# One decoder layer on one core: the residual's copy to DRAM in four pieces on the weights' queue, adding transfers in one half of down only, two results turned at other units

## The chip, the cores and the metric

One Trainium2 chip, of which the program uses one core. The metric is the device time of one execution in microseconds (us); the time of a kernel is the median of its timed runs.

## The reference, cut to what matters

The input is 256 tokens by 2048 numbers in float32. What matters here is the middle and the end of the layer: the residual `h` after attention, the SwiGLU block with its three weight matrices, and the gated block behind it.

```python
h = h + jnp.concatenate([out_mla, out_moba], axis=-1) @ w_o[i]

f = rmsnorm(h, ffn_norm[i])
h = h + (jax.nn.silu(f @ w_gate[i]) * (f @ w_up[i])) @ w_down[i]     # D_FF = 5632

g = jax.nn.sigmoid(rmsnorm(h, ple_norm[i]) @ w_ple_gate[i])
h = h + g * (p[i] @ w_ple_proj[i])
return rmsnorm(h, final_norm)
```

## The kernel before

**Products.** Every float32 operand is split into a high part (its value in the shorter format `fp32r`) and a low part (the rest), and a product is three matmuls (L342 to L344): high by high, low of the activations by high of the weights, high of the activations by low of the weights. The third one is the only one that reads the low part of the weights.

**Units and turns.** The work of TensorE is a list of units. A unit takes two blocks of 128 rows of a weight matrix by up to 1024 columns (1 MB). Some units have several turns. The groups of units come in this order: `wo0`, `wo1` (the product with `w_o`), then `g0`, `u0`, and for ci = 1 to 4 `g{ci}` (gate), `d{ci}0` (left half of the product with `w_down`, four units), `u{ci}` (up), `d{ci}1` (right half, four units), then `gu5`, `dl0`, `dl1` (the last piece of down, six units each) and the gated block (`pg`, `pe`). Five of the eight units of `g1` to `gu5` are done by Strassen's scheme in four turns, with seven products in place of eight and extra sums on VectorE (L330 to L334); `g1` and `u0` have fewer of these units.

**How a weight reaches TensorE.** SyncE's queue loads 1 MB into one of the buffers `raw` (L221), three of them until `wo1` and five after that: the fourth and the fifth lie where the attention results `oB` lie, which `wo1` reads to its end. ScalarE writes the high part from `raw` (`split_hi`, L317), VectorE the low part (`split_lo`, L325). Both go to a ring of places of 512 columns: 12 in the tiles `ringh`/`ringl`, 4 in `moreh`/`morel`, 4 in `most`. `plan` gives each split its places and the turn that read them last; the split is emitted right after that turn. `most` lies where `h` lies, so it may be used only while `h` is out of on-chip memory: from unit `wide + 8` (the first of `u0`; `wide` is the first of `g0`) up to `dl0`.

**The adding form of the low part.** For the unit with index 3 of each group of down, `split_hi` does something else: ScalarE writes the negative of `raw` into the low part's place (L315), a DMA on GpSimd's queue adds `raw` to it (L316), and ScalarE writes the high part. VectorE then has nothing to do for this unit.

```python
if units[jb.unit].adding:
    nc.scalar.mul(l, r, -1.0)
    nc.gpsimd.dma_start(l, r, accum_op=ALU.add)
nc.scalar.copy(h[:, :, c0:c1], r[:, :, c0:c1])
```

**The residual.** `h` is complete when `wo1` ends. `ffn_norm_half` scales it (L843), turns it with transposes on TensorE (L137) and splits it into `aT`, in steps between the units of `g0`. At the end of its second half a DMA on GpSimd's queue copies `h` (2 MB) to `hd` in DRAM (L863). Results of `d1` to `d4` are added to `hd` by DMAs on the same queue (L808), and `h` comes back in `dl0` (L993). GpSimd's queue also adds the Strassen sums to the gate's result (`stage<-U`, L903), once at the end of `g1` to `g4`, just ahead of the left half of down.

**Small steps.** `tasks` holds generators; at each even turn `step` runs those whose waiting count is over. The turned results of gate and up (`ff_transpose`, 8 transposes and two splits per step) are such a generator. For ci = 1 to 4 it is kept apart in `mid`, taken up when `d{ci}1` ends, and run at odd turns of the units that are not Strassen's: index 0 and index 1 of the next gate group.

Of the kernel before, what the change touches and what calls it, by code (L numbers as in the profile page):

```python
# [34 lines left out]
def kernel(ctx, tc, x, p, positions, attn_norm, w_in, kv_norm, w_ukv, w_o, ffn_norm,  # L35
                             w_gate, w_up, w_down, ple_norm, w_ple_gate, w_ple_proj, final_norm,
                             inv_freq, out):
    nc = tc.nc
# [162 lines left out]
    RING = 12  # L201
# [31 lines left out]
    def plan(wide):  # L233

        last, at = {}, 0

        def job(i, kind, kks, places):
            nonlocal at
            u, jb = units[i], Job()
            jb.unit, jb.kind, jb.kks, jb.turn, jb.first = i, kind, kks, len(turns), None  # L240
            if u.store:
                jb.wait = len(turns) - 3
            else:
                top = (RING + 8 if wide + 8 <= i < back else RING + 4) if u.deep else RING
                while at >= top or any(at < x < at + places for x in (RING, RING + 4)) or at + places > top:
                    at = 0 if at + 1 >= top else at + 1
                jb.first = at
                jb.wait = max(last.get(x, -1) for x in range(at, at + places))
                for x in range(at, at + places):
                    last[x] = len(turns)  # L250
                at += places
            jobs.append(jb)
            return jb

        order = [0, 1, 2]
        back = next(i for i, u in enumerate(units) if u.name == "dl0")
        for i, u in enumerate(units):
            u.turns = []
            if u.again:
                continue  # L260
            if i == wide + 3:
                order = [3, 4] + order
            u.raw = order.pop(0)
            order.append(u.raw)
            nch, nk = len(u.chunks), len(u.ks)
            if u.strassen:
                todo = [[("11 22", (0,), 2)], [("21", (0,), 1)], [("t3 t1", (0,), 2)], [("t2 t4", (0,), 2)]]
            elif u.store or u.adding or not u.mixed:
                todo = [[("", tuple(range(nk)), nk * nch)]]
            else:  # L270
                todo = [[("", (kk,), nch)] for kk in range(nk)]
                if u.last:
                    todo = [[x for y in todo for x in y]]
            for t in todo:
                u.turns.append([job(i, *x) for x in t])
                turns.append(i)
# [139 lines left out]
    def add(gen, wait=0, front=False):  # L416
        tasks.insert(0 if front else len(tasks), [wait, gen])
# [143 lines left out]
    S = {"done": 0, "doneB": 0}  # L561
# [23 lines left out]
    def stage_tile(n):  # L585
        return big.tile([128, NT, n], F32, name="stage", tag="stage")
# [240 lines left out]
    def ffn_norm_half(k0):  # L827

        def after():
            def g():  # L830
                if k0 == 0:
                    S["nrm"] = stage_tile(1024).rearrange("q t (a b) -> q (t a) b", a=2).rearrange(
                        "q n (u v) -> q n u v", u=2)
                    S["sums"] = big.tile([128, 2, 4, 3, 128], F32R, name="sums", tag="att")
                    if SEVENS > 4:
                        S["sums4"] = big.tile([128, 2, SEVENS - 4, 3, 128], F32R, name="sums4", tag="tabs")
                    S["s4"] = big.tile([128, 2, 128], F32, name="s4", tag="vb")
                    S["s4b"] = big.tile([128, SEVENS - 2, 128], F32, name="s4b", tag="mask")
                    S["rs"] = make_rstd(ssh[:, :, 0:2], D // 2, "rs")
                    yield 1  # L840
                def scale(k):
                    for t in range(NT):
                        nc.scalar.mul(S["nrm"][:, (k // 2) % 2, t], S["h"][:, t, k * 128:k * 128 + 256], S["rs"][:, t:t + 1])  # L843

                scale(k0)
                if k0:
                    scale(k0 + 2)
                yield 1
                for k in range(k0, k0 + 8, 2):
                    sums = [*(sums_of(k, i) for i in range(2)), S["s4"][:, k // 2] if k < 4 else S["s4b"][:, k // 2 - 2]] if k // 2 < SEVENS else None  # L850
                    act_transpose(S["h"], k, G_FFN, aT, scaled=True, sums=sums)
                    nx = k + (4 if k0 else 2)
                    if nx < k0 + 8:
                        scale(nx)
                    if k == 8:
                        rf = make_rstd(ssh, D, "rf0")
                        S["rf"] = const.tile([128, NT], F32, name="rf")
                        nc.vector.reciprocal(S["rf"], S["rs"])
                        nc.vector.tensor_tensor(S["rf"], S["rf"], rf, op=ALU.mult)
                    yield 1  # L860
                if k0:
                    S["hd"] = dram.tile([128, NT, D], F32, name="hd")
                    nc.gpsimd.dma_start(S["hd"], S["h"])  # L863
            add(g(), 1 if k0 == 0 else 0)
        return after

# [44 lines left out]
    def up_evac(ci, n, nb):  # L911
        left = {"n": nb}

        def f(c, t, c0, c1, b, off=0):
            st = S["ff"][:, t, c0 - off:c1 - off]
            nc.vector.scalar_tensor_tensor(st, b, S["rf"][:, t:t + 1], st, op0=ALU.mult, op1=ALU.mult)
            left["n"] -= 1
            if left["n"] == 0:
                if ci == 0:
                    fourth_sums(2, 4)  # L920
                turned = ff_transpose(ci, n, S.pop("ff"))
                if 0 < ci < 5:
                    S["turned"] = turned
                else:
                    add(turned, 1)
        return f

    def ff_transpose(ci, n, st):
# [48 lines left out]
    def down(k0, k1, name, ss=None, after=(None, None), halves=(0, 1)):  # L977
        for hc in halves:
            group(f"{name}{hc}", [(wd, hc * 1024, hc * 1024 + 1024)], list(range(k0, k1)), C2, ff_l,
                  (add_evac(hc * 1024, ss, after[hc]) if ss is not None else add_later(hc * 1024, after[hc])), swap=True, deep=True, adding=(3,))  # L980

    for ci in range(5):
        gate(ci)
# [117 lines left out]
    for t in range(NT):  # L1101
        for i in range(4):
            if t:
                u = Unit()
# [8 lines left out]
    wide = next(i for i, u in enumerate(units) if u.name == "g0")  # L1113
# [23 lines left out]
    for i, u in enumerate(units):  # L1137
        asking[0] = i
        load(i + 3)
        if i < 5:  # L1140
            load_x(xt, 768 + 256 * i, 1024 + 256 * i)
        if u.name == "dl0" and u.idx == 1:
            h_back()
        if u.name == "dl0" and u.idx == 2:
            add(p_load())
        for n in range(max(1, len(u.turns))):
            todo = []
            while nxt < len(jobs) and jobs[nxt].wait < j and jobs[nxt].unit <= i + 3 and \
                    (jobs[nxt].unit <= i + 2 or i >= wide and units[jobs[nxt].unit].asked < i):
                todo.append(jobs[nxt])  # L1150
                nxt += 1
            summed = [jb for jb in todo if jb.kind in ("t3 t1", "t2 t4") and
                      any(x.unit == jb.unit and x.kind in ("11 22", "21") for x in todo)]
            ahead = [jb for jb in todo if jb not in summed] if i >= 5 else []
            for jb in ahead:
                split_hi(jb)
            if n % 2 == 0:
                step()
            elif "mid" in S and not u.strassen and next(S["mid"], 0) == 0:
                S.pop("mid")  # L1160
            for jb in todo:
                if i < 3:
                    for c0, c1 in units[jb.unit].chunks:
                        split_hi(jb, c0, c1, len(jb.kks))
                        split_lo(jb, c0, c1, len(jb.kks))
                    continue
                if jb not in ahead:
                    split_hi(jb)
                split_lo(jb)
            while posts:  # L1170
                posts.pop()()
            done = jobs[nxt].unit - 1 if nxt < len(jobs) else len(units)
            for m in range(i + 4, min(done + 6, len(units)) if i >= wide else min(done + 4, wide + 3)):
                load(m)
            if u.strassen:
                seven(u, n)
            else:
                product(u, [kk for jb in u.turns[n] for kk in jb.kks] if u.turns else range(len(u.ks)))
            j += not u.again
# [25 lines left out]
```

## Time and profile before

| what | value |
|---|---|
| median of 3 runs | 1219.49 us (1218.84 to 1220.87) |
| the profiled execution's own time | 1215.02 us |
| its span, from first to last instruction | 1213.2 us |
| mean granted TensorE clock | 0.994 |
| TensorE matmul busy | 1189.3 us, 98% of the span |
| VectorE, ScalarE busy | 858.5 us (71%), 696.7 us (57%) |

The span is 1.8 us shorter than the profiled execution's own time, which holds what lies before the first and after the last instruction. Busy shares are averages over the whole span; a matmul's recorded duration overlaps the next one's, so its start-to-start distance says more than its busy time.

### The profile page before, as it was taken

The numbers are of one execution on the slowest core, as the hardware profiler recorded it, in microseconds if no ns is written. First come the engines' busy times: TensorE is split into PE (matmuls) and PEld (weight loads), VectorE is DVE, ScalarE is ACT, GpSimd is POOL, SyncE is SP. The second block draws the span as 40 slices with busy tenths as digits, with TensorE's granted clock in tenths as the row PEclk, the third lists the DMA queues.
The fourth block names the chain that finished last, engine by engine and source line by source line (L and its number), as shares of the span: only waits on it lengthen the run. The fifth ranks groups of instructions, "written<-read, shape, count | busy, mean of one in ns | idle before, by whom it ended". The sixth has DMA issues, their size and how long they took to land.

```text
span 1213.2 us, 14530 instructions
## 1 busy us (share of the span) xinstructions
PE 1189.3 (98%) x5582; PEld 1001.8 (83%) x5582; DVE 858.5 (71%) x1032; ACT 696.7 (57%) x871; POOL 47.1 (4%) x63
## 2 busy tenths in 40 slices
PE   9999999999999899999999999999999999999996
PEld 6999988899888688888888788888887888788885
DVE  5654635666457578968988798879897989555474
ACT  6744745456556564565656564756475745555453
POOL 5200000000000000000000000000000000000000
PEclk9999999999999899999999999999999999999998
DMA  9565554436564856386858777787769695884531
GB/s 310 167 205 171 174 174 139 149 119 218 174 242 151 310 195 247 123 280 221 288 163 265 255 243 220 245 267 247 235 213 272 228 259 189 296 285 140 208 104 69
DMA packets 79653, 256.59 MB, mean 211 GB/s; under 512 B 4892, under 2 KB 9296, under 8 KB 77408
## 3 DMA queue, kind: packets, MB, share of 16 engines
q1 hardware_dynamic: 74656, 227.83, 53.2%
q0 software_dynamic: 4640, 27.32, 10.7%
q8 instruction: 43, 0.70, 0.2%
q10 hardware_dynamic: 288, 0.52, 0.1%
q14 instruction: 26, 0.21, 0.0%
HBM read 228.39 MB, written 12.58 MB: 199 GB/s over the span
## 4 chain that ended last, share of the span: by engine, by line
PE 81%; issue 9%; DMA 7%; DVE 2%; ACT 1%; SPq 0%; POOL 0%; POOLq 0%; DVEq 0%; ACTq 0%
PE bank L344 26%; PE bank L342 25%; PE bank L343 25%; DMA ringl<-raw 3%; DMA morel<-raw 1%; DMA raw<-in_w_gate 1%; PE bank L503 1%; PE bank L137 1%; PE bank L624 1%; PE bank L532 1%; DMA h<-in_x 1%; DMA raw<-in_w_in 1%; PE bank L526 0%; PE bank L938 0%; PE bank L506 0%
## 5 line engine op out<-in xcount | busy, mean ns | idle before, releaser
L317 ACT CAST ringh<-raw 128x2048 fp32r<-128x2048 f32 (+5 forms) x274 | 351.9, 1309 | 298.6 <-PE bank L343 179.3
L325 DVE TENSOR_TENSOR ringl<-raw,ringh 128x1024 fp32r<-128x1024 f32 (+5 forms) x268 | 405.9, 1527 | 150.1 <-ACT ringh L317 145.5
L342 PE MATMUL bank<-ringh,aT 128*128 128x512 f32 (+3 forms) x779 | 296.3, 380 | 0.0
L344 PE MATMUL bank<-ringl,aT 128*128 128x512 f32 (+3 forms) x779 | 291.3, 374 | 2.7 <-DVE ringl L325 2.7
L343 PE MATMUL bank<-ringh,aT 128*128 128x512 f32 (+3 forms) x779 | 291.3, 374 | 0.8 <-DVE aT L124 0.8
L344 PEld LDWEIGHTS bank<-ringl,aT 128*128 128x128 f32 x779 | 146.7, 188 | 25.8 <-DVE ringl L325 3.2
L343 PEld LDWEIGHTS bank<-ringh,aT 128*128 128x128 f32 x779 | 146.8, 188 | 23.2 <-DVE aT L124 1.5
L342 PEld LDWEIGHTS bank<-ringh,aT 128*128 128x128 f32 x779 | 146.9, 189 | 22.5 <-ACT aT L123 0.7
L344 PE MATMUL bank<-ringl,ffTh 128*128 128x512 f32 x224 | 87.5, 391 | 4.6 <-DMA ringl<-raw 4.6
L325 DVE TENSOR_TENSOR morel<-raw,moreh 128x1024 fp32r<-128x1024 f32 (+2 forms) x58 | 75.3, 1321 | 22.7 <-ACT moreh L317 17.5
L317 ACT CAST moreh<-raw 128x1024 fp32r<-128x1024 f32 (+2 forms) x62 | 71.5, 1181 | 34.2 <-DVE raw L334 9.2
L342 PE MATMUL bank<-ringh,ffTh 128*128 128x512 f32 x224 | 87.4, 390 | 0.0
L343 PE MATMUL bank<-ringh,ffTl 128*128 128x512 f32 x224 | 87.2, 389 | 0.0
L317 ACT CAST most<-raw 128x1024 fp32r<-128x1024 f32 (+2 forms) x57 | 59.2, 1058 | 38.7 <-DVE raw L331 19.5
L325 DVE TENSOR_TENSOR most<-raw,most 128x1024 fp32r<-128x1024 f32 (+2 forms) x57 | 68.9, 1228 | 4.7 <-ACT most L317 4.5
L344 PEld LDWEIGHTS bank<-ringl,ffTh 128*128 128x128 f32 x224 | 42.0, 188 | 14.5 <-DMA ringl<-raw 5.9
L342 PE MATMUL bank<-moreh,aT 128*128 128x512 f32 x127 | 49.7, 391 | 0.0
L344 PE MATMUL bank<-morel,aT 128*128 128x512 f32 x127 | 49.4, 389 | 0.0
L343 PE MATMUL bank<-moreh,aT 128*128 128x512 f32 x127 | 49.4, 389 | 0.0
L343 PEld LDWEIGHTS bank<-ringh,ffTl 128*128 128x128 f32 x224 | 42.1, 188 | 8.7
L342 PEld LDWEIGHTS bank<-ringh,ffTh 128*128 128x128 f32 x224 | 42.0, 188 | 8.6
L342 PE MATMUL bank<-most,aT 128*128 128x512 f32 x110 | 43.1, 392 | 0.0
(293 smaller groups left out, 1802.9 us busy)
## 6 DMA issues: line engine op xcount, KB each, us to landing
raw<-in_w_down SPq DMA_DIRECT2D x44, 1024.0 KB, 4.9
raw<-in_w_gate SPq DMA_DIRECT2D x40, 1024.0 KB, 6.7
raw<-in_w_up SPq DMA_DIRECT2D x40, 1024.0 KB, 7.0
raw<-in_w_in SPq DMA_DIRECT2D x32, 512.0 KB, 4.2
raw<-in_w_o SPq DMA_DIRECT2D x16, 1024.0 KB, 5.0
raw<-in_w_ple_gate SPq DMA_DIRECT2D x16, 1024.0 KB, 4.9
raw<-in_w_in SPq DMA_DIRECT2D x16, 768.0 KB, 4.2
hd<-copied POOLq DMA_DIRECT2D x8, 1024.0 KB, 9.7
```

The source lines that it names most:

```text
L137: nc.tensor.transpose(b[:, (2 * i + t) * 128:(2 * i + t + 1) * 128], part[:, t, i * 128:(i + 1) * 128], ident)
L317: nc.scalar.copy(h[:, :, c0:c1], r[:, :, c0:c1])
L325: tt(l[:, :, c0:c1], r[:, :, c0:c1], h[:, :, c0:c1].bitcast(F32), op=ALU.subtract)
L342: nc.tensor.matmul(b, xh, h, start=start, stop=False)
L343: nc.tensor.matmul(b, xl, h, start=False, stop=False)
L344: nc.tensor.matmul(b, xh, l, start=False, stop=stop)
L503: nc.tensor.matmul(s[:, c0:c0 + nk], qT[:, q * 128:(q + 1) * 128], kT[:, 0:nk], start=True, stop=qpe is None)
L532: nc.tensor.matmul(o[:, 0:256], v(0), pT[:, 0:256], start=True, stop=False)
L624: nc.tensor.transpose(b[:, (2 * i + t) * 128:(2 * i + t + 1) * 128], src[:, t, col(i0 + i):col(i0 + i) + 128], ident)
```

## The change

Four edits. `h` goes to `hd` in four DMAs of 512 columns each on SyncE's queue, one per step, the first one two steps after the end of the second half. `most` may be used from unit `wide + 14` (the seventh of `u0`) on. The adding form stays in the right halves `d11` to `d41` alone: the left halves `d10` to `d40` and both groups of `dl` lose it. `ff_transpose` of `gu5` starts one step later, and `mid` may also run at even turns, except at the very first turn of the group.

```diff
-                top = (RING + 8 if wide + 8 <= i < back else RING + 4) if u.deep else RING
+                top = (RING + 8 if wide + 14 <= i < back else RING + 4) if u.deep else RING
...
                 if k0:
                     S["hd"] = dram.tile([128, NT, D], F32, name="hd")
-                    nc.gpsimd.dma_start(S["hd"], S["h"])
+                    yield 2
+                    for n in range(4):
+                        nc.sync.dma_start(S["hd"][:, :, n * 512:n * 512 + 512], S["h"][:, :, n * 512:n * 512 + 512])
+                        yield 1
...
                 if 0 < ci < 5:
                     S["turned"] = turned
                 else:
-                    add(turned, 1)
+                    add(turned, 2 if ci else 1)
...
     def down(k0, k1, name, ss=None, after=(None, None), halves=(0, 1)):
...
-                  (add_evac(hc * 1024, ss, after[hc]) if ss is not None else add_later(hc * 1024, after[hc])), swap=True, deep=True, adding=(3,))
+                  (add_evac(hc * 1024, ss, after[hc]) if ss is not None else add_later(hc * 1024, after[hc])), swap=True, deep=True,
+                  adding={0: (), 1: (3,)}[hc] if name != "dl" else ())
...
             if n % 2 == 0:
                 step()
-            elif "mid" in S and not u.strassen and next(S["mid"], 0) == 0:
+            if "mid" in S and not u.strassen and 2 * u.idx + n > 0 and next(S["mid"], 0) == 0:
                 S.pop("mid")
```

SyncE's queue at the loads of `u0` and `g1` (the `raw` numbers are buffers), with the rows that go and come:

```order
 L221 DMA raw_2891<-in_w_up 128x2x1024
 L221 DMA raw_2899<-in_w_up 128x2x1024
-L221 DMA raw_112<-in_w_up 128x2x1024
+L865 DMA hd<-h 256x1x512 x2
+L221 DMA raw_112<-in_w_up 128x2x1024
+L865 DMA hd<-h 256x1x512 x2
 L221 DMA raw_113<-in_w_gate 128x2x1024
 L221 DMA raw_114<-in_w_gate 128x2x1024
```

The four pieces stand around the load of the last unit of `u0`; the two loads ahead of them are those of its sixth and seventh unit.

GpSimd's queue before, from the copy of `h` to the end of the second block of down (`L316` is the adding form, `L903` the sum for the gate, `L808` a result of down):

```order
L863 DMA hd<-h 128x4096
L903 DMA stage<-U 128x2048
L316 DMA ringl<-raw_114 128x2048
L808 DMA hd<-copied 256x1x1024
L316 DMA morel<-raw_2899 128x2048
L808 DMA hd<-copied 256x1x1024
L903 DMA stage<-U 128x2048
L316 DMA ringl<-raw_113 128x2048
L808 DMA hd<-copied 256x1x1024
L316 DMA ringl<-raw_2891 128x2048
L808 DMA hd<-copied 256x1x1024
```

The same queue of the change over the same stretch (`L906` is what was `L903`):

```order
L906 DMA stage<-U 128x2048
L808 DMA hd<-copied 256x1x1024
L316 DMA ringl<-raw_2899 128x2048
L808 DMA hd<-copied 256x1x1024
L906 DMA stage<-U 128x2048
L808 DMA hd<-copied 256x1x1024
L316 DMA ringl<-raw_2891 128x2048
L808 DMA hd<-copied 256x1x1024
```

The copy of `h` is gone from it, and so is the adding form that stood right behind each sum for the gate; the one between two results of down stays.

ScalarE at the start of `d20` before (the copies to `stage` are the gate's result):

```order
L898 COPY stage<-bank_81 128x512
L898 COPY stage<-bank_82 128x512
L315 ACTIVATE ringl<-raw_113 128x2048
L317 CAST ringh<-raw_113 128x2048
L317 CAST ringh<-raw_114 128x1024 x2
```

ScalarE at the same place of the change (`L901` is what was `L898`):

```order
L901 COPY stage<-bank_81 128x512
L901 COPY stage<-bank_82 128x512
L317 CAST moreh<-raw_113 128x2048
L317 CAST most<-raw_114 128x1024 x2
L317 CAST ringh<-raw_2891 128x1024 x2
```

The negative copy is gone, the high parts follow one another, and they stand at other places of the ring; VectorE gets one more low part of 128x2048 behind them.

## Rows read from the trace of the kernel before

**Rows 1.** The head and the first part of the page: the span, and for each engine busy us, share of the span and number of instructions.
```profile
span 1213.2 us, 14530 instructions
...
PE 1189.3 (98%) x5582; PEld 1001.8 (83%) x5582; DVE 858.5 (71%) x1032; ACT 696.7 (57%) x871; POOL 47.1 (4%) x63
```

**Rows 2.** The waits of TensorE over the whole span, the three longest: who was waited for, us in total, times, longest.
```profile
PE bank L344 <- DMA ringl<-raw: 4.6, 3, 2.0
PE bank L137 <- ACT stage L843: 2.9, 1, 2.9
PE bank L344 <- DVE ringl L325: 2.7, 1, 2.7
```

**Rows 3.** TensorE's instructions in order of time around the start of the fourth unit of `g0`: start, us, what, and in brackets the idle time before it with what ended it.
```profile
404.65 0.39 PE L343 MATMUL bank<-ringh,aT 128*128 128x512 f32 x1
404.88 0.39 PE L344 MATMUL bank<-ringl,aT 128*128 128x512 f32 x1
408.15 0.95 PE L137 MATMUL bank<-ident,stage 128*128 128x128 f32 x4 [2.88 <-ACT stage L843]
...
409.16 0.41 PE L343 MATMUL bank<-ringh,aT 128*128 128x512 f32 x1
412.31 0.79 PE L344 MATMUL bank<-ringl,aT 128*128 128x512 f32 x1 [2.73 <-DVE ringl L325]
```

**Rows 4.** Two stretches around it: from and to, length, busy time of TensorE, its weight loads, VectorE, ScalarE and GpSimd with the number of instructions, granted TensorE clock, busy share of the DMA engines, GB/s.
```profile
394.00:403.00 9.00, 9.00 (x43) 7.41 (x42) 0.00 (x0) 2.51 (x2) 0.00 (x0) 1.00 0.99 408
412.30:416.30 4.00, 3.99 (x10) 3.15 (x11) 3.46 (x4) 1.42 (x4) 0.00 (x0) 0.51 0.71 242
```

**Rows 5.** ScalarE and VectorE in order of time in the same place (columns as in rows 3).
```profile
402.40 1.91 ACT L317 CAST moreh<-raw 128x2048 fp32r<-128x2048 f32 x1 [6.39 <-DMA raw<-in_w_gate]
...
407.59 0.90 ACT L843 ACTIVATE stage<-h,rs 128x256 f32<-128x256 f32 x2
...
409.97 2.28 DVE L325 TENSOR_TENSOR ringl<-raw,ringh 128x2048 fp32r<-128x2048 f32 x1
```

**Rows 6.** The copy of `h`: its issue on GpSimd (start, us of issuing, what, idle before it), and its row in the list of DMA issues (size, us from issue to landing).
```profile
388.98 0.62 POOL L863 DMA_DIRECT2D hd<-h  x1 [227.23 <-DVE h L789]
...
hd<-h POOLq DMA_DIRECT2D x1, 2048.0 KB, 14.1
```

**Rows 7.** Single loads, each from the list of DMA issues of the window in which it was issued, with size and us to landing: those issued at 387.98 and 388.40 us, then three issued at 540.17, 540.63 and 541.21 us.
```profile
raw<-in_w_gate SPq DMA_DIRECT2D x1, 1024.0 KB, 6.0
raw<-in_w_gate SPq DMA_DIRECT2D x1, 1024.0 KB, 13.9
...
raw<-in_w_up SPq DMA_DIRECT2D x1, 1024.0 KB, 4.9
raw<-in_w_up SPq DMA_DIRECT2D x1, 1024.0 KB, 7.0
raw<-in_w_up SPq DMA_DIRECT2D x1, 1024.0 KB, 9.0
```

**Rows 8.** GpSimd's instructions in order of time, in the second block of down: two at the start of `d20`, one in `d21` (columns as in rows 6).
```profile
653.17 0.87 POOL L903 DMA_DIRECT2D stage<-U  x1 [41.08 <-DVE U L410]
654.72 0.86 POOL L316 DMA_DIRECT2D ringl<-raw  x1 [0.67 <-ACT ringl L315]
...
716.78 0.87 POOL L316 DMA_DIRECT2D ringl<-raw  x1 [39.68 <-ACT ringl L315]
```

**Rows 9.** TensorE in order of time where it waits for an adding DMA, in `d20` and in `d30`: the matmul before the wait, the one after it, and for `d20` the next (columns as in rows 3).
```profile
668.37 0.39 PE L343 MATMUL bank<-ringh,ffTl 128*128 128x512 f32 x1
669.80 0.50 PE L344 MATMUL bank<-ringl,ffTh 128*128 128x512 f32 x1 [1.05 <-DMA ringl<-raw]
670.14 0.40 PE L342 MATMUL bank<-ringh,ffTh 128*128 128x512 f32 x1
...
795.26 0.39 PE L343 MATMUL bank<-moreh,ffTl 128*128 128x512 f32 x1
795.72 0.50 PE L344 MATMUL bank<-morel,ffTh 128*128 128x512 f32 x1
```

**Rows 10.** What the two forms of the low part cost: VectorE's instruction on 128x2048 and ScalarE's negative copy, each as a group (count, busy us, mean ns, idle before it), and VectorE in order of time in `d20`.
```profile
L325 DVE TENSOR_TENSOR ringl<-raw,ringh 128x2048 fp32r<-128x2048 f32 x81 | 185.0, 2287 | 71.8 <-ACT ringh L317 71.8
L315 ACT ACTIVATE ringl<-raw 128x2048 fp32r<-128x2048 f32 x6 | 11.5, 1920 | 5.1 <-PE bank L344 5.1
...
657.19 4.63 DVE L325 TENSOR_TENSOR ringl<-raw,ringh 128x1024 fp32r<-128x1024 f32 x4 [2.35 <-ACT ringh L317]
```

**Rows 11.** VectorE's last split for `g4` and TensorE's first matmul of the unit that reads it.
```profile
897.43 1.22 DVE L325 TENSOR_TENSOR morel<-raw,moreh 128x1024 fp32r<-128x1024 f32 x1
...
899.22 0.39 PE L342 MATMUL bank<-ringh,aT 128*128 128x512 f32 x1
```

**Rows 12.** Two stretches with the columns of rows 4: `d20`, and the Strassen units of `g4`.
```profile
650.00:675.00 25.00, 23.95 (x106) 19.52 (x105) 16.36 (x18) 14.44 (x17) 1.73 (x2) 1.00 0.91 268
872.00:899.00 27.00, 27.00 (x125) 22.47 (x124) 25.00 (x30) 15.50 (x18) 0.00 (x0) 1.00 0.39 132
```

**Rows 13.** What stands where the four pieces go in `u0`: the issue of the load of its last unit on SyncE, ScalarE's first split of that load, and from the list of DMA issues four transfers of 512 KB issued one behind the other (size, median us to landing).
```profile
438.20 0.37 SPq L221 DMA_DIRECT2D raw<-in_w_up  x1
...
458.59 1.05 ACT L317 CAST ringh<-raw 128x1024 fp32r<-128x1024 f32 x1
...
h<-in_x SPq DMA_DIRECT2D x4, 512.0 KB, 8.0
```

## The prediction

> **What bounds the kernel now.** The page comes first: TensorE's matmuls are busy for 98% of the span [rows 1], so time can be won only where TensorE stands still, and lost only where something new makes it stand still. The waits of TensorE say where that is, and there are few [rows 2]: three waits for an adding DMA (`ringl<-raw`), one for ScalarE's scaling in `ffn_norm_half` (L843), one for a low part from VectorE. The rest of the table is start-up.
>
> TensorE's own rows then give each loss. Its matmuls of 512 columns start 0.23 us apart (404.65 to 404.88). In the fourth unit of `g0` the distance is 3.27 us once and 3.15 us once [rows 3], so 3.0 and 2.9 us are lost. Behind the second one the granted clock is 0.51 for 4.0 us, the lower level of 1.2 GHz, after two stops of about 3 us within 8 us: 10 matmuls take 3.99 us there [rows 4] where 10 x 0.23 = 2.3 are normal, another 1.7 us. **g0 loses 7.7 us in all.**
>
> At the adding DMAs, `d20` shows 1.43 us between starts (1.20 lost) and 0.34 us for the next one (0.11 lost): 1.31 for a listed idle time of 1.05, so 0.26 more than listed [rows 9]. The three listed waits sum to 4.6 [rows 2], which makes 4.6 + 3 x 0.26 = 5.4. `d30` has a fourth one too short for the list: 0.46 - 0.23 + 0.11 = 0.34. **The adding form loses 5.7 us.**
>
> **Why g0 waits.** Backwards: the low part that TensorE lacks is written at 409.97 to 412.25; ScalarE's scaling for the late transposes at 407.59; both stand in order behind one split that idled 6.39 us for its load and started at 402.40 [rows 5]. That load was issued at 388.40 and took 13.9 us; the one just ahead took 6.0 [rows 7]. GpSimd issued the 2 MB copy of `h` at 388.98, and it landed after 14.1 us, at 403.1 [rows 6]: beside the late load all the way. The DMA engines were 99% busy then, at 408 GB/s [rows 4]. Where three loads are issued as closely with no such copy, they land after 4.9, 7.0 and 9.0 us [rows 7].
>
> **Part 1: the copy of `h` moves to SyncE's queue.** What counts is when the pieces run. On GpSimd's queue nothing stood ahead of the copy, so it started as soon as `h` was complete. On SyncE's queue it stands behind the loads of the sixth and seventh unit of `u0`, which wait for buffers. So it leaves the stretch 388 to 408. How early does the late load land then? By the nearest rows, 7.0 us after its issue, at 395.4. The other bound takes only the copy's 2.1 MB out at 408 GB/s: 5.1 us earlier, 397.2. ScalarE's split moves from 402.40 to 395.4 or 397.2, and what follows it in order moves along by 7.0 or 5.2 us. The scaling ends at 401.5 or 403.3 in place of 408.49; TensorE wants it at 405.1: the first stop is gone by either bound. The low part ends at 405.3 or 407.1; TensorE reaches it at 405.1 + 1.0 (transposes and first matmul, 408.15 to 409.16) + 0.2 = 406.3: gone, or 0.8 us left. Without two long stops I expect no lower clock: `d20` stops for 1.2 us and its window shows 1.00 [rows 12]. I take the nearer rows, so 7.7 us are won; the other bound leaves 6.9.
>
> The Trainium skill speaks against this part: "DMA: Bandwidth & Descriptors", section "Issuing engines are not separate DMA queues", says that transfers started by any engine run on the same 16 DMA engines and interleave, so another queue saves only issuing time. The 13.9 beside 7.0 us agree. By that rule alone the 7.7 us stay lost and the time would be 1213.8.
>
> What do the pieces meet in `u0`? Two go ahead of the load of its last unit, issued at 438.20; that load lands some 5 us later, at 443, and is first split at 458.59 [rows 13]: 15.5 us of cover. Four transfers of 512 KB behind one another have a median of 8.0 us; taken one at a time, far too high, the two ahead of the load cost 16 us, half a microsecond over the cover. The lower bound is 2.1 MB at 408 GB/s, 5.1 us for all four. The two behind it end at 443 + 16 = 459 at the latest, when the first split into `most` wants the old `h` gone. TensorE waits for nothing in `u0` today [rows 2], so half a microsecond there costs nothing. I take 0, at most 0.6.
>
> `most` coming six units later leaves `u0` a ring of 16 places in place of 20. The shortest distance from a place's last reader to its new reader becomes 36 matmuls, 36 x 0.23 = 8.2 us; a split of 1024 columns needs a ScalarE copy and a VectorE instruction of 1.22 us [rows 11], some 2.5 us with the handing over. Cost 0. Later on the same 20 places are used from another start: the first splits of `u1`, `g2`, `u2`, ... begin at places 12, 16, 4, 12, ... before and 4, 12, 16, 4, ... after, the same three cases in turn.
>
> **Part 2: no adding form in the left halves and in `dl`.** In `d20` the adding DMA is issued 1.6 us behind the sum for the gate [rows 8] and lands only when TensorE is waiting; `d30` and `d40` repeat this, and in `dl0` the neighbour is the copy of `h` back. All four waits are of these kinds, and the six transfers behind them go: 5.7 us won. The right halves keep theirs; in `d21` GpSimd had idled 39.68 us before it [rows 8], and no right half is in the waits.
>
> The price: six more VectorE instructions of 2.29 us, against six ScalarE copies of 1.92 us saved [rows 10]. In `d20` VectorE is busy for 16.4 of 25 us [rows 12], and it sits 2.35 us idle just there, behind the negative copy that goes [rows 10]: the new instruction fits into that hole. In `dl` each unit lasts 24 x 0.23 = 5.5 us and wants one instruction of 2.29. Cost 0; what it costs uncovered is rival A.
>
> **Part 3: the turned results.** Same transposes and splits, at other units. For `gu5` one unit later, with `ffT` first read in the fifth unit of `dl0`, two units (11 us) behind its new place; for `g2` to `gu5` half of it one turn earlier. TensorE waits for neither today [rows 2]. Cost 0, no gain taken: a VectorE that does it earlier may gain margin at most.
>
> **The sum.** 7.7 + 5.7 = 13.4 us off the profiled execution's own 1215.0 (its span is 1213.2) gives 1201.6. The median shown is 4.5 us above that execution, so 1219.5 - 13.4 = **1206.1**.
>
> **Rivals.**
> A. *VectorE gives it back.* In the Strassen units of `g4` VectorE is busy 25.0 of 27.0 us [rows 12], and its last split ends at 898.65, 0.57 us before TensorE's first matmul there at 899.22 [rows 11]. If the 2.29 us in `d10` to `d40` were carried into the following `u` group with no more margin than that, four times 2.29 - 0.57 = 1.7, 6.9 us, would come back: 1213.0. Against it: the hole of 2.35 us, and a ring that lets VectorE run no further ahead.
> B. *g0 waits all the same*, because the loads hinder one another or the pieces collide elsewhere: only the 5.7 us are won, 1213.8. Against it: 4.9, 7.0, 9.0 us.
> C. *Slower: the rotated ring breaks the thin margins.* There are nine Strassen groups from `g1` to `gu5`. If the new places cost each M us of margin, 9 x (M - 0.57) is lost; from M = 2.1 on that is 13.4, and at M = 3 it is 22 us: 1228. Against it: the three starting places are the same.
> D. *It does not do what it says*: the pieces run as early as the copy did and the freed adding slots are filled by another late DMA. No change, 1219. Against it: the queue's order.
>
> **Chances.** The forecast 0.62 (1204 to 1208); A in part or whole 0.16 (1208 to 1213); B 0.09; D 0.05; C 0.04; 0.04 for more gain than the sum. Faster 0.91, same 0.05, slower 0.04, where 0.2% (2.4 us) is about what measuring this kernel can tell from no change. The range 1203.5 to 1212 holds the forecast and most of A, about 8 in 10.
>
> **What would show it.** The late load of `g0` lands about 7 us after its issue, and no wait on L843 or L325 is left in `g0`, with a granted clock of 1.00 around 412 us; were the load early and the stop still there, the chain behind ScalarE is misread. Waits of TensorE for `ringl<-raw` are gone. New waits on L325 at the ends of `u1` to `u4` would show A, at all nine group ends C. A load of `u0` or `g1` landing after ScalarE wants it would show the pieces in the way.

## The result and the profile after

The changed kernel takes 1201.53 us (median of 4 executions, 1201.47 to 1201.67); the kernel before 1219.16 us (median of 4, 1217.38 to 1220.87: the three runs of the table of before and one more). The ratio is 0.9856, with a 95% interval of 0.9839 to 0.9873. The forecast was 1206.1 in a range of 1203.5 to 1212: the sign was right, the gain larger than forecast, and the time lies 2 us below the range.

The profiled execution of the changed kernel takes 1201.50 us. Against the profiled execution of before (1215.02) that is 13.5 us less, and the sum of the prediction was 13.4. The median moved by 17.6. So what is to be explained is less the sum than the way from it to a median. The executions of the changed kernel lie within 0.2 us, those of before within 3.5 us.

The head and first part of the page after, to be read beside [rows 1]:

```profile
span 1199.7 us, 14518 instructions
...
PE 1186.0 (99%) x5582; PEld 1001.5 (83%) x5582; DVE 871.6 (73%) x1038; ACT 685.9 (57%) x865; POOL 42.0 (4%) x56
```

TensorE's waits after, all that are listed (columns as in [rows 2]); the first one is start-up:

```profile
PE bank L112 <- DVE junk L107: 2.0, 1, 2.0
PE bank L344 <- DVE ringl L325: 0.8, 1, 0.8
PE bank L342 <- DVE h L789: 0.3, 1, 0.3
PE bank L343 <- DVE aT L124: 0.3, 1, 0.3
```

The three waits of [rows 2] are gone but for 0.8 us. TensorE in order of time in the same place of `g0` (to be read beside [rows 3]):

```profile
405.03 0.60 PE L137 MATMUL bank<-ident,stage 128*128 128x128 f32 x4
405.38 0.48 PE L342 MATMUL bank<-ringh,aT 128*128 128x512 f32 x1
405.69 0.40 PE L343 MATMUL bank<-ringh,aT 128*128 128x512 f32 x1
406.87 0.50 PE L344 MATMUL bank<-ringl,aT 128*128 128x512 f32 x1 [0.78 <-DVE ringl L325]
```

The transposes run without a wait. The low part is still missed once: 1.17 us between starts in place of 0.23, 0.94 lost. In the window of [rows 4] behind it the granted clock is 1.00 in place of 0.51, and 20 matmuls start in place of 10:

```profile
412.30:416.30 4.00, 4.00 (x20) 3.31 (x19) 3.18 (x4) 3.23 (x5) 0.00 (x0) 1.00 0.98 336
```

ScalarE and VectorE after, in order of time (the rows that answer to [rows 5]):

```profile
396.95 1.91 ACT L317 CAST moreh<-raw 128x2048 fp32r<-128x2048 f32 x1 [2.05 <-DMA raw<-in_w_gate]
...
402.16 0.91 ACT L843 ACTIVATE stage<-h,rs 128x256 f32<-128x256 f32 x2
...
404.53 2.28 DVE L325 TENSOR_TENSOR ringl<-raw,ringh 128x2048 fp32r<-128x2048 f32 x1
```

And from the list of DMA issues the late load (issued at 388.32), and the four pieces (issued between 426.6 and 439.8), each with size and us to landing:

```profile
raw<-in_w_gate SPq DMA_DIRECT2D x1, 1024.0 KB, 8.6
...
hd<-h SPq DMA_DIRECT2D x4, 512.0 KB, 8.6
```

The late load takes 8.6 us in place of 13.9 [rows 7], ScalarE splits it at 396.95 in place of 402.40, and the chain behind it moves by 5.4 us.

The same matmuls can be set against each other in both profiles, since their number is the same. From 404 to 430 us the changed kernel gains 7.2 us (`g0`), at the adding waits of `d20`, `d30`, `d40` and `dl0` another 5.9; the prediction had 7.7 and 5.7.

### The profile page after: what moved, and what is told of

It is laid out like the page before. It is cut to its first block, busy times and chain, and to the rows that moved or that the text cites. A ratio compares the mean times of both kernels' runs of the same rounds, so it can differ in the third digit from the quotient of the medians.

```text
span 1199.7 us, 14518 instructions
## 1 busy us (share of the span) xinstructions
PE 1186.0 (99%) x5582; PEld 1001.5 (83%) x5582; DVE 871.6 (73%) x1038; ACT 685.9 (57%) x865; POOL 42.0 (4%) x56
## 4 chain that ended last, share of the span: by engine, by line
PE 95%; DMA 2%; DVE 1%; ACT 1%; SPq 0%; issue 0%; DVEq 0%; ACTq 0%
PE bank L344 30%; PE bank L343 30%; PE bank L342 30%; PE bank L503 1%; PE bank L941 1%; PE bank L137 1%; DMA raw<-in_w_gate 1%; PE bank L624 1%; PE bank L532 1%; DMA h<-in_x 1%; DMA raw<-in_w_in 1%; PE bank L526 0%; PE bank L506 0%; PE bank L533 0%; DVE ringl L325 0%
## 5 line engine op out<-in xcount | busy, mean ns | idle before, releaser
L325 DVE TENSOR_TENSOR ringl<-raw,ringh 128x1024 fp32r<-128x1024 f32 (+5 forms) x273 | 414.6, 1534 | 144.5 <-ACT ringh L317 138.4
L317 ACT CAST ringh<-raw 128x1024 fp32r<-128x1024 f32 (+5 forms) x276 | 353.8, 1308 | 284.2 <-PE bank L343 168.2
L342 PE MATMUL bank<-ringh,aT 128*128 128x512 f32 (+3 forms) x810 | 308.0, 380 | 0.0
L344 PE MATMUL bank<-ringl,aT 128*128 128x512 f32 (+3 forms) x810 | 302.7, 374 | 0.8 <-DVE ringl L325 0.8
L343 PE MATMUL bank<-ringh,aT 128*128 128x512 f32 (+3 forms) x810 | 302.9, 374 | 0.3 <-DVE aT L124 0.3
L344 PEld LDWEIGHTS bank<-ringl,aT 128*128 128x128 f32 x810 | 152.2, 188 | 24.8 <-DVE ringl L325 1.2
L343 PEld LDWEIGHTS bank<-ringh,aT 128*128 128x128 f32 x810 | 152.4, 188 | 23.8 <-DVE aT L124 0.9
L342 PEld LDWEIGHTS bank<-ringh,aT 128*128 128x128 f32 x810 | 152.4, 188 | 23.2 <-ACT aT L123 0.5
L325 DVE TENSOR_TENSOR morel<-raw,moreh 128x1024 fp32r<-128x1024 f32 (+2 forms) x62 | 83.3, 1358 | 20.0 <-ACT moreh L317 19.4
L342 PE MATMUL bank<-moreh,aT 128*128 128x512 f32 x115 | 45.0, 392 | 0.0
L343 PE MATMUL bank<-moreh,aT 128*128 128x512 f32 x115 | 44.8, 389 | 0.0
L344 PE MATMUL bank<-morel,aT 128*128 128x512 f32 x115 | 44.8, 389 | 0.0
L124 DVE SCALAR_TENSOR_TENSOR aT<-bank,gain,aT 128x256 fp32r<-128x256 f32 x38 | 18.1, 482 | 25.8 <-ACT aT L123 25.7
```

The costliest lines, as they stand in the source:

```text
L124: nc.vector.scalar_tensor_tensor(lo, ps, scale, hi.bitcast(F32), op0=ALU.mult, op1=ALU.subtract)
L325: tt(l[:, :, c0:c1], r[:, :, c0:c1], h[:, :, c0:c1].bitcast(F32), op=ALU.subtract)
L342: nc.tensor.matmul(b, xh, h, start=start, stop=False)
L343: nc.tensor.matmul(b, xl, h, start=False, stop=False)
L344: nc.tensor.matmul(b, xh, l, start=False, stop=stop)
```

## The experiments

Two theories for the gain above the sum. Theory 1: the stretch around `g0`, with the 2 MB copy beside the weight loads, costs more in other executions of before than in the profiled one. Theory 2: the waits for adding DMAs do. All times in one table (median, range and number of executions; the clock is the mean granted TensorE clock of the executions):

| kernel | us | clock |
|---|---|---|
| before again | 1217.91 (1214.98 to 1222.89, 12) | 0.989 to 0.995 |
| part 1 alone | 1207.02 (1206.37 to 1209.08, 4) | 0.997 to 0.998 |
| part 2 alone | 1209.58 (1208.47 to 1210.84, 5) | 0.992 to 0.995 |
| parts 1 and 2 | 1203.60 (1203.39 to 1204.75, 4) | 0.997 to 0.998 |
| ring only | 1216.14 (1213.89 to 1218.85, 10) | 0.992 to 0.995 |
| parts 1, 2 and the later turn of `gu5` | 1201.19 (1201.14 to 1201.84, 4) | 0.997 to 0.998 |
| pieces early | 1211.90 (1210.67 to 1212.84, 10) | 0.991 to 0.994 |
| low part first | 1201.01 (1200.46 to 1201.63, 4) | 0.997 to 0.998 |
| before, two looks | 1219.68; 1219.95 | 0.992; 0.992 |
| after again | 1201.41 (1201.16 to 1201.87, 4) | 0.997 to 0.998 |
| low part first, without the earlier turns | 1200.72 (1200.49 to 1201.84, 4) | 0.997 to 0.998 |

Beside the first four, the kernel before took 1217.41 us (17 executions), beside the next four 1216.86 (19), beside the last four 1218.71 (7). Each of these three sets was timed on one chip of the same kind, each set on another chip. On the third, where the two looks were taken too, none of nine executions of before was shorter than 1216.96 us; on the other two the shortest took 1214.98 and 1214.65 us. How much of before's scatter belongs to the chip was not tested. The changed kernel took 1201.53 and, on the third chip, 1201.41.

### Before again, and the two parts alone

The kernel before, with no edit:

> The kernel before, unchanged, to see where its other executions lose more than the profiled one did (its executions took 1217.4 to 1220.9 us, its profiled one 1215.0; the changed kernel's all took 1201.5 to 1201.7). Both theories: about 1219, over 1 us between the executions. Theory 1 (the stretch around g0, with the 2 MB copy beside the weight loads, varies): if this profile is again slower than 1215.0, the added time stands in the fourth unit of g0 (more than 7.7 us lost there), and the adding waits stay at 5.7 us. Theory 2 (the waits for adding DMAs vary): g0 stays at 7.7 us and the waits for ringl after adding DMAs sum to 8 to 12 us. Should the profile be near 1215 again, it tells nothing between them, and the scatter of the two kernels with one part each decides.

Part 1 alone (the two edits of `top` and of the copy, as in the diff of the change):

> Part 1 alone: the copy of h in four pieces on SyncE's queue, and most six units later; the adding form stays everywhere. Theory 1 (what varies is the stretch around g0): all of it goes, 1201.5 + 5.7 = 1207.2, with executions within 0.5 us of each other. Theory 2 (the adding waits vary): 1219.2 - 7.7 = 1211.5, with executions scattered over some 3 us as before. Both: no long stop in g0 and a granted clock of 1.00 around 412 us.

Part 2 alone:

```diff
+                  adding={0: (), 1: (3,)}[hc] if name != "dl" else ())
```

> Part 2 alone: no adding form in the left halves of down and in dl; the copy stays on GpSimd's queue. Theory 1: 1219.2 - 5.7 = 1213.5, with executions scattered over some 3 us as before. Theory 2: 1201.5 + 7.7 = 1209.2, with executions within 0.5 us of each other. Both: the two stops of about 3 us in g0 stay, and no wait for an adding DMA is left.

Before again was profiled in one of its short executions (1215.54) and shows what the first profile showed: 4.7 us of listed waits for `ringl<-raw`, 2.8 and 2.4 in `g0`. Its twelve executions reach from 1214.98 to 1222.89, so the profiled 1215.02 was near the low end and the three timed runs, 1218.84 to 1220.87, near the upper one.

Part 1 alone came out as theory 1 expects in its median (1207.0, ratio 0.9916, 0.9901 to 0.9930), part 2 alone as theory 2 expects (1209.6, ratio 0.9934, 0.9921 to 0.9947). Neither is as steady as its theory wants: 2.7 and 2.4 us between executions. So each part alone gains more than the sum has for it (7.7 and 5.7), and each leaves something that varies. Part 2 alone was profiled in the longest of its executions. Two of its windows, with the columns of [rows 4]:

```profile
412.00:416.00 4.00, 2.94 (x7) 2.36 (x8) 3.60 (x3) 0.36 (x1) 0.00 (x0) 0.50 0.41 116
416.00:420.00 4.00, 4.00 (x12) 3.10 (x12) 3.17 (x3) 3.45 (x6) 0.00 (x0) 0.59 1.03 407
```

The half clock lasts until about 419 us here, and 13 matmuls start 0.43 us apart; in the profile of before it lasts until about 416, and seven do. The first stop is 3.57 us between starts in place of 3.27, the second 2.63 in place of 3.14. Between the starts of the same matmuls this execution loses 8.6 us more in `g0` than the profiled execution of the changed kernel, where before's profile loses 7.2 more. That is most of the 9.3 us between the two executions (1210.84 and 1201.50); 0.5 of the rest lies ahead of `g0`. By the medians the difference is 8.1.

### Two looks at before

No edit; two single executions with their traces.

> The kernel before, unchanged: another execution with its trace, to see where a longer one loses. Theory 1: if it takes more than 1217 us, the half clock behind the stops of g0 lasts longer than the 6.7 us (granted clock under 1.00 from 408 to 417) of the executions of 1213.9 to 1215.5 us: 10 us or more, and the stops there are no shorter. Theory 2: the half clock is as long as there, and the waits for adding DMAs are longer. At about 1215 it tells nothing.

> The kernel before once more, with the same question and the same numbers as the look beside it.

Both caught longer executions. TensorE in the second look, in order of time: the adding wait in `d20`, then the one in `dl0` (to be read beside [rows 9]):

```profile
669.10 0.39 PE L343 MATMUL bank<-ringh,ffTl 128*128 128x512 f32 x1
671.80 0.50 PE L344 MATMUL bank<-ringl,ffTh 128*128 128x512 f32 x1 [2.31 <-DMA ringl<-raw]
...
673.37 0.63 PE L344 MATMUL bank<-ringl,ffTh 128*128 128x512 f32 x1
673.80 0.63 PE L342 MATMUL bank<-ringh,ffTh 128*128 128x512 f32 x1
...
1052.76 0.39 PE L343 MATMUL bank<-ringh,ffTl 128*128 128x512 f32 x1
1055.23 0.60 PE L344 MATMUL bank<-ringl,ffTh 128*128 128x512 f32 x1 [2.08 <-DMA ringl<-raw]
1055.64 0.63 PE L342 MATMUL bank<-ringh,ffTh 128*128 128x512 f32 x1
```

The stop in `d20` is 2.70 us between starts in place of 1.43, and some matmuls later starts are 0.43 us apart (673.37 to 673.80): the half clock, which `d20` does not have in the profile of before [rows 12]. `dl0` shows the same. Two windows of this look, with the columns of [rows 4]:

```profile
673.30:675.30 2.00, 2.00 (x6) 1.54 (x5) 0.00 (x0) 0.31 (x1) 0.00 (x0) 0.50 0.82 311
...
1055.20:1058.50 3.30, 3.27 (x8) 2.58 (x9) 1.53 (x1) 0.00 (x0) 0.00 (x0) 0.54 0.59 191
```

What is late is the adding DMA itself. Issued in `d20` at 655.45, its row in the list of DMA issues of the second look is

```profile
ringl<-raw POOLq DMA_DIRECT2D x1, 1024.0 KB, 16.3
```

and in the profile of before, issued at 654.72,

```profile
ringl<-raw POOLq DMA_DIRECT2D x1, 1024.0 KB, 15.0
```

A load of 1 MB issued beside it on SyncE's queue took 16.3 and 15.2 us (16.6 in the first look, as long as the adding DMA there), so it is not the adding form alone that is late; what delays both was not found.

The waits of TensorE in the first look:

```profile
PE bank L344 <- DMA ringl<-raw: 6.2, 3, 2.6
PE bank L137 <- ACT stage L843: 3.3, 1, 3.3
...
PE bank L344 <- DMA morel<-raw: 1.0, 1, 1.0
```

Its adding wait in `d20`, 2.94 us between starts:

```profile
668.94 0.39 PE L343 MATMUL bank<-ringh,ffTl 128*128 128x512 f32 x1
671.88 0.50 PE L344 MATMUL bank<-ringl,ffTh 128*128 128x512 f32 x1 [2.56 <-DMA ringl<-raw]
```

Where the looks part from the profile of before, read from the starts of the same matmuls: the first look is ahead by 0.33 us before `g0`, 0.57 us behind at the stop of `d20`, and 4.7 behind at the end. So `g0` costs 0.9 us more, and the adding waits with the half clock behind them 4.1 us more (1.5 at `d20`, 0.9 at `d30`, nothing at `d40`, 1.7 at `dl0`, of which 1.6 at the half clock). In the second look it is level before `g0`, 0.73 behind at `d20` and 4.9 at the end: 0.8 in `g0`, 4.2 for the adding waits (the two stretches at the half clock are 1.6 each).

The stretch of `g0` in the profile of before, in the first look and in the second, with the columns of [rows 4]:

```profile
404.00:420.00 16.00, 10.31 (x40) 7.65 (x39) 12.03 (x23) 9.90 (x17) 0.00 (x0) 0.79 0.70 260
...
404.00:420.00 16.00, 10.70 (x35) 7.72 (x34) 11.94 (x23) 9.53 (x17) 0.00 (x0) 0.68 0.66 240
...
404.00:420.00 16.00, 9.68 (x34) 7.09 (x33) 11.43 (x22) 9.88 (x17) 0.00 (x0) 0.79 0.66 247
```

A mean clock of 0.79 over 16 us makes 6.7 us at the half clock, 0.68 makes 10.2. So the sign of theory 1, 10 us or more, shows in the first look alone, and there the second stop is shorter (2.63 us between starts in place of 3.14); in the second look the half clock is as long as before, and the first stop is longer (3.90 in place of 3.27). **`g0` brings under a fifth of what these two executions lose beyond the profile of before, the waits for adding DMAs the rest: theory 2 has by far the larger share.** In these executions the adding form costs 5.7 + 4.1 or 4.2 = about 9.9 us, not 5.7.

### The ring, and the result of `gu5`

Parts 1 and 2 without part 3:

> Parts 1 and 2 together, without part 3 (the two results are turned where they were before). The prediction's step: part 3 is worth nothing, 1201.5 (within 0.5). Rival: part 3 is what gives the gain above the forecast, then this is at the 1206 that was forecast, and the waits that are back show where.

1203.60 (ratio to before 0.9888, 0.9872 to 0.9904): part 3 is worth 2.1 us, and the rival's side is the right one. TensorE in this kernel at the end of `gu5`, where `L941` turns its result:

```profile
1026.48 0.27 PE L941 MATMUL bank<-ident,stage 128*128 128x128 f32 x1
1028.55 0.98 PE L941 MATMUL bank<-ident,stage 128*128 128x128 f32 x7 [1.80 <-DVE stage L919]
```

The profile of before has no such wait. VectorE in order of time there, first in this kernel (`L410` and `L372` are the last Strassen sums, `L919` writes the result):

```profile
1021.33 0.68 DVE L410 TENSOR_TENSOR U<-U,bank 128x512 f32<-128x512 f32 x1
1021.93 2.29 DVE L325 TENSOR_TENSOR ringl<-raw,ringh 128x2048 fp32r<-128x2048 f32 x1
1024.13 1.28 DVE L372 TENSOR_TENSOR U<-U,bank 128x512 f32<-128x512 f32 x2
...
1027.74 0.75 DVE L919 SCALAR_TENSOR_TENSOR stage<-U,rf,stage 128x512 f32<-128x512 f32 x1 [0.19 <-ACT stage L892]
```

and then before, where `L919` is `L916`:

```profile
1032.19 0.68 DVE L410 TENSOR_TENSOR U<-U,bank 128x512 f32<-128x512 f32 x1
1032.79 1.28 DVE L372 TENSOR_TENSOR U<-U,bank 128x512 f32<-128x512 f32 x2
...
1036.40 0.75 DVE L916 SCALAR_TENSOR_TENSOR stage<-U,rf,stage 128x512 f32<-128x512 f32 x1 [0.20 <-ACT stage L889]
1038.20 2.29 DVE L325 TENSOR_TENSOR ringl<-raw,ringh 128x2048 fp32r<-128x2048 f32 x1 [1.05 <-ACT ringh L317]
```

A split of 2.29 us that stood behind the result stands ahead of the last sums now, and the result comes that much later. Whether the ring does it:

```diff
-                top = (RING + 8 if wide + 8 <= i < back else RING + 4) if u.deep else RING
+                top = (RING + 8 if wide + 14 <= i < back else RING + 4) if u.deep else RING
```

> The kernel before with most coming six units later and nothing else changed. Theory: the other ring brings in a wait of its own. In the run with parts 1 and 2 TensorE waits 1.8 us for VectorE at the end of gu5 (two starts 2.07 us apart), because a split of 2.29 us stands ahead of the last additions there. Then this kernel has that wait too: 1217.4 + 1.8 = 1219.2 (executions scatter by some 2 us, so the trace decides, not the time). Rival: the wait comes from the copy's new place, then this kernel has no wait at the end of gu5 and takes the 1217.4 of before. If my step of the prediction on the ring was right (cost 0), the rival holds.

It does. The trace of this kernel has the wait, and the split ahead of the sums, with the copy where it was. TensorE's waits in it, two rows:

```profile
PE bank L344 <- DMA ringl<-raw: 1.9, 2, 0.9
PE bank L938 <- DVE stage L916: 1.5, 1, 1.5
```

Its time missed the expectation all the same (ratio 0.9989, 0.9972 to 1.0006, where 1.8 us more were expected): the same ring shortens the adding waits in sum. Between starts they are 1.00, 1.31 and 1.32 us in `d20`, `d30` and `d40` in place of 1.43, 0.46 and 1.93 (the one in `d30` is longer), and the one in `dl0` (2.39) is gone, where the adding DMA now lands after 8.0 us in place of 11.6. Why it lands sooner was not followed further. It is also one reason why the parts don't add up: alone they win 10.4 and 7.8 us, together 13.8. Part 1 alone holds the ring's edit too, and its trace has the ring's wait at the end of `gu5` (1.5 us) and no adding wait in `dl0`. So its 10.4 us are not those of the copy alone, and what it says for theory 1 is weaker by that; the copy moved without the other ring was not run.

Which edit of part 3 it is (parts 1 and 2 with this one alone):

```diff
-                    add(turned, 1)
+                    add(turned, 2 if ci else 1)
```

> Parts 1 and 2 and of part 3 only the result of gu5 turned one unit later; the result of g2 to gu5 is not turned earlier. Theory: the whole of part 3's 2.1 us is the wait at the end of gu5: 1201.5, as the changed kernel. Rival: the earlier turning brings part of it: 1202 to 1203.

1201.19, the time of the changed kernel: the later turn of `gu5` is all of part 3, the earlier turns of `g2` to `gu5` are worth nothing that can be measured.

### The same queue at the early time

```diff
                 if k0:
                     scale(k0 + 2)
+                    S["hd"] = dram.tile([128, NT, D], F32, name="hd")
+                    for n in range(4):
+                        nc.sync.dma_start(S["hd"][:, :, n * 512:n * 512 + 512], S["h"][:, :, n * 512:n * 512 + 512])
                 yield 1
```

The later place of the four pieces is taken out.

> The changed kernel, but its four pieces stand on SyncE's queue where h is complete, ahead of the second of the loads issued together in g0, as early as GpSimd's copy was. Theory 1 (when the copy runs is what counts, not whose queue it is on): the late load lands at 401 to 403, g0 stops twice again and loses 7 to 9 us: 1208.5 to 1210.5. Theory 2 (SyncE's queue or the four pieces are what helps): the late load lands at about 397 and the time is 1201.5 to 1202.

1211.90: theory 1, and beyond its numbers. TensorE at the first stop of `g0` in this kernel:

```profile
405.56 0.39 PE L344 MATMUL bank<-ringl,aT 128*128 128x512 f32 x1
410.39 1.30 PE L137 MATMUL bank<-ident,stage 128*128 128x128 f32 x4 [4.44 <-ACT stage L843]
```

The stop is 4.83 us between starts in place of 3.27 [rows 3], because on this queue the late load stands behind the pieces: issued at 392.18 in place of 388.40, landed at 404.56 in place of 402.3. Its row in the list of DMA issues:

```profile
raw<-in_w_gate SPq DMA_DIRECT2D x1, 1024.0 KB, 12.4
```

Queue and pieces are those of the changed kernel; what differs is their place in the queue (and that they follow one another at once), and 10.4 us with it. When the pieces run is what helps.

### What is left in `g0`

In the changed kernel VectorE starts the low part that TensorE misses at 404.53, though its high part was ready at 394.9: it stands in order behind the work on the late transposes and on `rf`. Moved ahead:

```diff
             for jb in ahead:
                 split_hi(jb)
+            first_lo = ahead[0] if u.name == "g0" and u.idx == 1 and ahead else None
+            if first_lo:
+                split_lo(first_lo)
```

> The changed kernel with one VectorE instruction moved: in the second unit of g0 the first low part (it starts at 404.53 in the changed kernel's trace, with its high part ready since 394.9) goes ahead of the work on the late transposes and on rf. Theory: the stop of 0.94 us that is left in g0 (two starts 1.17 us apart) is this place in VectorE's order, not the load: 1201.5 - 0.9 = 1200.6. Rival: it is the load, or the transposes come later by what the low part takes: 1201.5 or up to 1202.5.

VectorE in this kernel, where it had idled, and TensorE at the old stop:

```profile
395.81 2.29 DVE L325 TENSOR_TENSOR ringl<-raw,ringh 128x2048 fp32r<-128x2048 f32 x1 [1.38 <-ACT ringh L317]
400.90 0.69 DVE L121 TENSOR_TENSOR aT<-stage,aT 128x512 fp32r<-128x512 f32 x1 [2.81 <-ACT aT L120]
```

```profile
406.31 0.40 PE L343 MATMUL bank<-ringh,aT 128*128 128x512 f32 x1
406.54 0.40 PE L344 MATMUL bank<-ringl,aT 128*128 128x512 f32 x1
```

The stop is gone, 0.23 us between starts. The time of 1201.01 is less clear, since in the profiled execution the start-up took 0.8 us longer than in that of the changed kernel. So once more beside the changed kernel, together with the earlier turns taken back:

> The changed kernel, unchanged, beside the next one: 1201.5, its executions within 0.5 us.

> The changed kernel with the low part moved ahead in the second unit of g0, and without the earlier turning of g2 to gu5, which was worth nothing. Theory: no stop of TensorE over 0.5 us behind the start-up, so 0.9 us less than the changed kernel beside it: 1200.6. Rival: what the start-up takes differs from execution to execution by as much, and the two can't be told apart.

1200.72 against 1201.41, 0.7 less by the medians; the ranges overlap. The waits are gone, and between the same matmuls `g0` is 1.0 us shorter in the trace; in the time this is at the edge of what these executions can tell. (The changed kernel's own four executions lie within 0.7 us, where 0.5 was expected.)

## Why the prediction was wrong in its time and right in most of its steps

**Why `g0` waits, and the copy moved: right in mechanism.** The late load landed after 8.6 us, between the bounds of 7.0 (the nearer rows, which I took) and 8.8 and close to the upper one. The 0.94 left is the "0.8 us left" of that bound. The 7.7 itself was a little small: from the starts of the same matmuls `g0` loses 8.3 us in the profile of before, of which 7.2 were won. The sum had left out the transposes behind the first stop, which start more slowly (408.15 to 409.16 in place of 405.03 to 405.69), and took ten distances where the starts from 412.31 to 416.29 have nine. And it does not take two stops: in the first look the mean clock is 0.80 over 406 to 408 us, when TensorE still stands in its first stop, and 0.50 over the next two. The rule of the Trainium skill that I set against this part ("DMA: Bandwidth & Descriptors", section "Issuing engines are not separate DMA queues": transfers of all issuers share 16 engines) agrees with the early pieces, which cost no less on SyncE's queue (1211.90) than the copy did on GpSimd's (part 2 alone, 1209.58). What I drew from it as rival B did not follow: the change moves the transfer in time too, and at 426.6 to 439.8 us there was room.

**The pieces in `u0`: right.** They landed after 8.6 us in the median where 8.0 was taken, and no wait appeared in `u0`.

**`most` six units later, cost 0: wrong in the changed kernel.** I looked at how near a reader comes to the reuse of a place, and at the starting places of the groups. I did not look at what a different sequence of places does to the order on VectorE: one split goes ahead of the last sums of `gu5`, and TensorE waits 1.8 us. The order of the changed kernel on VectorE shows this without a run.

**Part 3, cost 0 and no gain: right as a sum, wrong as a reason.** "TensorE waits for neither today" was true of before and not of the kernel with parts 1 and 2. Its 2.1 us cancel the cost of the ring; two errors of about the same size stood on the two sides, and that they cancel is luck.

**The adding form, 5.7 us: the term that was too small.** That is its size in the profiled execution (5.9 from the starts). In two others it was about 9.9, since the adding DMA of `d20` lands 1.3 us later or more, and since the clock fell there behind single stops of 2.5 to 2.7 us. "Without two long stops I expect no lower clock" came true for `g0` of the changed kernel, whose stop of 0.94 us is followed by 1.00; as a rule it does not hold.

**The last step: the one that failed.** "The median shown is 4.5 us above that execution, so 1219.5 - 13.4" takes the 4.5 us for something that the change leaves alone. In the two longer executions that were traced, the added 4.7 and 4.9 us are made of the very losses that the change removes. The three runs that gave the 4.5, besides, lie high: 55 other executions of before, in four sets, have medians of 1216.9 to 1218.7. Without `g0`'s stops and the adding waits little is left to vary (1201.16 to 1201.87 in eight executions), and the changed kernel's median is its profiled time. The sum against the profiled execution's own time, 1201.6, stood in the sentence before, and the range left it out. That it meets the 1201.53 so closely is in part luck, since it took 0.5 us too much for `g0`, 0.2 too little for the adding form, and nothing for the 0.4 by which the two executions differ elsewhere.

Rivals A and D did not come, and C only in one of its nine places: there is no wait at the ends of `u1` to `u4`, and at no group's end but `gu5`'s. That one comes from the ring, as C says, but by an order and not by a margin, and the later turn covers it.

## What to carry to other kernels

When the profiled execution is shorter than every timed one, the stalls it shows may be short ones, as here: price the sum against its own time as well, and let the range hold both results. When an edit shifts the places that a planner gives out, compare the order on every engine over the whole program, not only the distance between a place's users; and an edit that seems to cost and win nothing may be there to cover another one, so price it in the kernel that has the others. What the copy cost here was decided by when it ran and what stood behind it, on either queue.

## What the runs showed of the hardware that was not expected

A stop of about the same length can be followed by the half clock or not, and a longer one need not be. In `d20`, 2.94 us between starts left the granted clock at 1.00 in the first look, while 2.70 us were followed by the half clock in the second; in `dl0`, 2.39 us (before) and 2.57 us (before again) were not followed by it, 2.54 and 2.47 us (the looks) were. Why was not found. The stop in `dl0` of the profile of before:

```profile
1049.48 0.39 PE L343 MATMUL bank<-ringh,ffTl 128*128 128x512 f32 x1
1051.88 0.50 PE L344 MATMUL bank<-ringl,ffTh 128*128 128x512 f32 x1 [2.00 <-DMA ringl<-raw]
```

Two windows of the first look, behind its stop in `d20`, with the columns of [rows 4]; the second one is where the second look had 0.50:

```profile
671.80:674.00 2.20, 2.12 (x9) 1.77 (x10) 0.00 (x0) 0.59 (x1) 0.00 (x0) 1.00 0.45 69
674.00:676.00 2.00, 2.00 (x10) 1.64 (x10) 0.00 (x0) 0.73 (x2) 0.00 (x0) 1.00 0.99 403
```

The Trainium skill ("TensorE: Matmul & The Clock Gate", section "HAM oscillation — how this bites in real kernels") tells of a kernel whose long waits for DMA between groups of matmuls bring the clock down, so that each next group starts at the lower clock. The second look agrees, and there it costs 1.6 us a time, more than half as much again as the stop itself; the stop of 2.94 us in the first look shows that it need not follow. And the same adding DMA of 1 MB landed after 15.0, 16.6 and 16.3 us in `d20` of three executions of one program.
